# Expert rows by indirect transfers instead of one-hot products, in the first expert stage of a two-block kernel

## The chip, the cores and the metric

The kernel is one program on one core of a Trainium2 chip. The core has a matrix engine (TensorE, PE in the rows; its weight loads are shown as PEld), three elementwise engines (VectorE or DVE, ScalarE or ACT, GpSimd or POOL), a queue engine (SyncE or SP) that issues most transfers, and 16 DMA engines that all queues share. The metric is the device time of one execution in microseconds, as the median of several runs. It is compared with the time of the kernel before the change.

## The reference, cut to what matters

A block of 512 tokens of width 1024 goes through two network blocks one after the other. The first ends with an expert-choice layer: each of 16 experts picks the 64 tokens that its router column rates highest, runs them through a gated network of its own and adds the weighted result back to those tokens.

```
cap = CAP_FACTOR * l // N_EXPERTS                      # 2*512//16 = 64 rows an expert
aff = softmax(h @ w_router)                            # 512 x 16
vals, idx = lax.top_k(swapaxes(aff, 1, 2), cap)        # 16 x 64
xs = h[bidx, idx]
hid = silu(xs @ w_gate) * (xs @ w_up)                  # 64x1024 @ 1024x1024, for each expert
y = (hid @ w_down) * vals[..., None]
x = x + ga2 * zeros_like(h).at[bidx, idx].add(y)
```

Here `h` is the row-normalised `x`, then multiplied by a column scale and shifted (`gs2` and `sh2` in the kernel). The three weight matrices of an expert hold 4 MiB each, so the layer reads 192 MiB. Everything is in float32. The second block, with convolution, attention and another expert layer, follows and isn't touched.

## The kernel before, in words

The program is written as phases. Tiles are drawn from pools with a fixed number of buffers; a planner orders each engine's instructions ahead of time and gives out buffers as they come free in its plan, and each engine and the SP queue then run their lists in order.

`phase_a` computes the first block up to its two branches. `phase_a2` forms the residual `xres` (four tiles of 128 tokens by 1024), its row factors `rs[t]` (L235), the router logits (`logits`, L907 to L941), the 64 best tokens of each expert by eight rounds of max, replace and find index (L990 to L993), and the index and value columns `idxF` and `valF` (L1015, L1016). Keys and values of the second block's cross attention (`mem_k`, `mem_v`, products on L89 to L91) fill TensorE meanwhile. The working tiles of the logits, `xT` and `lgq`, come from a pool tag `ch` with six buffers.

`phase_b` is the first expert stage. Experts go in eight pairs, one in the upper and one in the lower 64 columns of the array, so a tile of rows is 128 rows of a pair. For pair p:

- `gather(p)`: `rows_b` spreads the pair's 128 indices over the partitions by a product (L1038) and compares them with the token numbers (L1041), which gives a one-hot matrix G whose ones carry the row factor `rs4`. A product of `xres` with G (L1079) gives the transposed, normalised rows; `scale_T` (L223) applies column scale and shift.
- `pair_mm` with gate, then up, then down weights (L1068; the last pair's down weights in `last_down`, L1096). Each weight chunk is 256 rows of one expert's matrix, a tile of 128 x 2 x 1024 float32, which is 1 MiB, loaded by L118 on the SP queue. Four steps of two chunks make one `pair_mm`; an expert pair needs 24 chunks and the stage 192.
- `hidden` (L1103 to L1107) multiplies and transposes, `scatter(p)` weights the result (L1122), splits it into a high and a low part (L1124, L1125), brings it back to token order by products with a one-hot matrix P (L96, L97) and adds it (L1130). The sums go into a tile `acc` of their own for pairs 0 to 6, since `gather` still reads `xres`; the last pair adds `acc` and its own rows into `xres`.

The chunks are held in 16 buffers that the loads take in turn: three each of `rawp`, `rawb` and `rawb2`, six of `rawb3`, one of `rawb4`. A load waits until the chunk that was in its buffer has been used. Nine chunks are asked for in `phase_a2` (`preload`), the others as buffers come free. `rawb4` lies on memory that `mem_v` uses until it ends. For the last pair, a tile `gg` for constants of the next phase takes one `rawp` buffer and keeps it.

Of the kernel before, what the change touches and what calls it, by code (L numbers as in the profile page):

```python
# [8 lines left out]
F32 = mybir.dt.float32  # L9
F32R = mybir.dt.float32r  # L10
U32 = mybir.dt.uint32
# [20 lines left out]
NRAW_B3 = 6  # L32
NRAW_B4 = 1
NRAW_D = 4
# [17 lines left out]
def host_constants():  # L52
    c = {}
    c["ident"] = np.eye(128, dtype=np.float32)
    p = np.arange(128)
    c["mask_f"] = np.where(p[:, None] > p[None, :], BIG, 0.0).astype(np.float32)
    c["mask_b"] = np.where(p[:, None] < p[None, :], BIG, 0.0).astype(np.float32)
    s2 = np.zeros((128, 2), np.float32)
    s2[0::32, 0] = 1.0
    s2[1::32, 1] = 1.0  # L60
    c["sel_two"] = s2
    def ang4(r):
        return 2.0 * np.pi * np.outer(p, 4 * p + r) / T
    co, si = (lambda r: np.cos(ang4(r))), (lambda r: np.sin(ang4(r)))
    c["dft_l"] = np.concatenate([co(0), si(0), co(2), si(2), co(1), co(3), si(1), si(3),
                                 -si(1), si(3), co(1), -co(3)], 1).astype(np.float32) * np.float32(T ** -0.5)
    ang = 2.0 * np.pi * np.outer(p, p) / 128
    c["dft_d"] = np.concatenate([np.cos(ang), -np.sin(ang)], 1).astype(np.float32) * np.float32(128 ** -0.5)
    c["mask_n"] = np.where(p[None, :] > p[:, None], -BIG, 0.0).astype(np.float32)
    c["tri"] = np.where(p[:, None] < p[None, :], 1.0, 0.0).astype(np.float32)  # L70
    small = np.zeros((128, 64), np.float32)
    small[:, 8:12] = np.array([4.0, 3.0, 2.0, 1.0])[None, :]
    place = (p[:, None] + 128 * np.arange(4)[None, :])[:, :, None, None] + np.zeros((1, 1, 2, 2))
    place[:, :, 1, 1] += T
    small[:, 16:32] = (place + 1.0).reshape(128, 16)
    c["small"] = small
    c["tokid"] = (p[:, None] + 128 * np.arange(4)[None, :]).astype(np.float32)
    c["iota"] = np.tile(np.arange(T, dtype=np.float32), (128, 1))
    return c


class Builder:
# [156 lines left out]
    def build(self):  # L239
        with ExitStack() as es:  # L240
# [9 lines left out]
            with ExitStack() as right:  # L250
                self.consts()
                with ExitStack() as pb:
                    self.open_b(pb)
                    late = self.phase_a(right)
                    G0 = self.phase_a2(late, pb, right)
                    self.phase_b(pb, right, G0)
                self.raws = [self.rawp] * NRAW
                with ExitStack() as pc:
                    self.phase_c(pc, right)
                with ExitStack() as pd:  # L260
                    self.phase_d(pd)
# [3 lines left out]

    def consts(self):
        nc, I, cst = self.nc, self.I, self.cst
        self.mhalf = cst.tile([128, 1], F32, name="mhalf")
        nc.gpsimd.memset(self.mhalf, -0.5)
        rows1 = cst.tile([128, 128], F32, name="rows1")  # L270
        nc.vector.memset(rows1, 0.0)
# [14 lines left out]

        t = cst.tile([128, 16], F32, name="csil_t")
        nc.scalar.activation(out=t, in_=self.cols1[:, 0:16], func=AF.Tanh, scale=0.5)
        t2 = cst.tile([128, 16], F32, name="csil_t2")
        nc.vector.scalar_tensor_tensor(t2, t, 1.0, self.cols1[:, 0:16], op0=OP.add, op1=OP.mult)  # L290
        self.csil = cst.tile([128, 8, 32], F32, name="csil")
        nc.vector.memset(self.csil, 0.0)
# [45 lines left out]
    def phase_a(self, right):  # L338
        tc, nc, I = self.tc, self.nc, self.I
        cst = self.cst  # L340
        ident = self.ident
        pa, pm, early, late = ExitStack(), ExitStack(), ExitStack(), ExitStack()
        hxp = self.pool(pa, "hxp", 12)
# [503 lines left out]
    def phase_a2(self, late, pb, right):  # L847
# [18 lines left out]
        nc.sync.dma_start(out=wr, in_=I["w_router"][0].rearrange("(k p) c -> p k c", p=128))  # L866
        self.rs4 = cst.tile([128, 4], F32, name="rs4")
        self.tokid = cst.tile([128, 4], F32, name="tokid")
        nc.sync.dma_start(out=self.tokid, in_=I["tokid"])
        affT = self.pa(256, name="affT")  # L870
# [90 lines left out]
        for t in range(4):  # L961
# [4 lines left out]
            ev_x(t, 1, ps)  # L966
            rs[t] = self.row_rstd(sm, sss[t], out=self.rs4[:, t:t + 1])
        logits()
# [41 lines left out]
        V.tensor_tensor(bidx, bidx, two[:, 3, 0:16], op=OP.add)  # L1010
        self.idxF = cst.tile([128, 8], F32, name="idxF")
        self.valF = cst.tile([128, 8], F32, name="valF")
        for par in range(2):
            o = slice(par * 64, par * 64 + 64)
            V.tensor_copy(self.idxF[o, :], bidx.rearrange("c (p two) -> c p two", two=2)[:, :, par])  # L1015
            V.tensor_copy(self.valF[o, :], best.rearrange("c (p two) -> c p two", two=2)[:, :, par])  # L1016
        mem_k()
        G0 = self.rows_b(0)
        mem_v()
        sms.close()  # L1020
        return G0

# [11 lines left out]
    def rows_b(self, p):  # L1034

        V, nc = self.nc.vector, self.nc
        ps = self.pa(128, name="bcI")
        nc.tensor.matmul(ps, self.idxF[:, p:p + 1].to_broadcast([128, 128]), self.ident, start=True, stop=True)  # L1038
        G = self.xsp.tile([128, 4, 128], F32, tag="G", name="G", bufs=1)
        for t in range(4):  # L1040
            V.tensor_scalar(G[:, t, :], ps, self.tokid[:, t:t + 1], self.rs4[:, t:t + 1], op0=OP.is_equal, op1=OP.mult)  # L1041
        return G

    def phase_b(self, pb, right, G0):
        tc, nc, I = self.tc, self.nc, self.I
        ident = self.ident
        V, AC = nc.vector, nc.scalar
        xp = self.pool(pb, "xp", 2)

        acc = xp.tile([128, 4, 1024], F32, name="acc", bufs=1)  # L1050
        if NRAW_B4:
# [18 lines left out]

        def gather(p):
            G = G0 if p == 0 else self.rows_b(p)
            xT = xp.tile([128, 8, 128], F32, tag="xT", name="xT")
            for e in range(2):
                ps = self.pa()
                for q in range(4):
                    k = 4 * e + q
                    for t in range(4):
                        nc.tensor.matmul(ps[:, q * 128:(q + 1) * 128], xres[:, t, k * 128:(k + 1) * 128], G[:, t, :], start=t == 0, stop=t == 3)  # L1079
                self.scale_T(xT[:, 4 * e:4 * e + 4, :].rearrange("p k s -> p (k s)"), ps, self.gs2, self.sh2, 4 * e)  # L1080
            return xT

# [33 lines left out]
        def scatter(p, py):  # L1116
# [3 lines left out]
            for e in range(2):  # L1120
# [5 lines left out]
                for t in range(4):  # L1126
                    ps = self.pa()
                    self.mm2(ps, P[:, t * 128:(t + 1) * 128], (H, L), True, True)
                    c = slice(e * 512, (e + 1) * 512)
                    V.tensor_tensor((acc if p < 7 else xres)[:, t, c], (acc if p else xres)[:, t, c], ps, op=OP.add)  # L1130


        xT = gather(0)
        nc.sync.dma_start(out=self.iota, in_=I["iota"])
# [3 lines left out]
        for p in range(8):  # L1138
            hid = silu(pg)
            nxt = gather(p + 1) if p < 7 else None  # L1140
            hT = hidden(hid, pair_mm(w_u, p, xT))
# [940 lines left out]
```

## Time and profile before

| what | value |
|---|---|
| median of 3 runs | 1710.59 us (1710.18 to 1715.16) |
| the profiled execution | 1714.91 us |
| its span in the profile | 1713.1 us |
| mean granted TensorE clock | 0.969 of full speed |
| busy: PE, DVE, ACT, POOL | 92%, 50%, 36%, 33% of the span |
| read from memory, written | 367.40 MB, 19.93 MB |

The span runs from the first to the last instruction of the profiled execution; 1.8 us of its time lie around it. Times in rows are microseconds from the span's start. The first expert stage runs from about 540 to 1024 us. A busy share of PE is not a share of its peak, because the ends of its pipelined matmuls are modelled. The granted clock is a share of 2.4 GHz, so 0.50 is 1.2 GHz. A float32 matmul of the program is two instructions in the rows.

### The profile page before, as it was taken

The numbers are of one execution on the slowest core, as the hardware profiler recorded it, in microseconds if no ns is written. First come the engines' busy times: TensorE is split into PE (matmuls) and PEld (weight loads), VectorE is DVE, ScalarE is ACT, GpSimd is POOL, SyncE is SP. The second block draws the span as 40 slices with busy tenths as digits, with TensorE's granted clock in tenths as the row PEclk, the third lists the DMA queues.
The fourth block names the chain that finished last, engine by engine and source line by source line (L and its number), as shares of the span: only waits on it lengthen the run. The fifth ranks groups of instructions, "written<-read, shape, count | busy, mean of one in ns | idle before, by whom it ended". The sixth has DMA issues, their size and how long they took to land. (4 is left out here: it accounts for less than half of the span.)

```text
span 1713.1 us, 20867 instructions
## 1 busy us (share of the span) xinstructions
PE 1579.9 (92%) x7702; PEld 1049.7 (61%) x7702; DVE 856.2 (50%) x1595; ACT 613.5 (36%) x1277; POOL 564.9 (33%) x447
## 2 busy tenths in 40 slices
PE   5988999999999999999999978999999989789994
PEld 3766667777776444344344337778666766566663
DVE  4388554423554122022202137997754463667776
ACT  3433354433432000000000034325763354467773
POOL 1213314344513000000000014575443342647765
PEclk9999999999999999999999988999999999889997
DMA  9522412364746999999999983322112328369944
GB/s 302 172 89 91 139 56 93 126 202 148 256 164 245 396 409 409 409 409 409 409 409 409 409 268 124 99 81 91 50 50 85 124 79 327 108 238 346 346 161 165
DMA packets 165548, 381.23 MB, mean 223 GB/s; under 512 B 16302, under 2 KB 74742, under 8 KB 165436
## 3 DMA queue, kind: packets, MB, share of 16 engines
q1 hardware_dynamic: 161116, 371.63, 59.0%
q0 software_dynamic: 4320, 8.16, 1.3%
q8 instruction: 63, 1.03, 0.3%
q14 instruction: 49, 0.40, 0.1%
HBM read 367.40 MB, written 19.93 MB: 226 GB/s over the span
## 5 line engine op out<-in xcount | busy, mean ns | idle before, releaser
L130 POOL TENSOR_TENSOR wL<-raw,wH 128x512 fp32r<-128x512 f32 x220 | 312.0, 1423 | 424.5 <-ACT wH L129 396.1
L129 ACT ACTIVATE wH<-raw 128x512 fp32r<-128x512 f32 x240 | 149.6, 628 | 256.8 <-PE ps L90 149.7
L1068 PE MATMUL ps<-raw,xT 128*64 128x512 f32 x1024 | 240.8, 595 | 0.0
L1068 PEld LDWEIGHTS ps<-raw,xT 128*64 128x64 f32 x1024 | 74.3, 137 | 137.3 <-issue 133.4
L1125 POOL TENSOR_TENSOR yL<-y,yH 128x512 fp32r<-128x512 f32 x14 | 17.9, 1278 | 419.4 <-ACT yH L1124 409.2
L1122 DVE SCALAR_TENSOR_TENSOR y<-ps,valF,ga 128x512 f32<-128x512 f32 x16 | 12.0, 751 | 228.0 <-PE ps L1068 206.8
L91 PE MATMUL ps<-raw,wL 128*128 128x512 f32 (+1 forms) x320 | 120.6, 377 | 2.9 <-POOL wL L130 2.9
L89 PE MATMUL ps<-raw,wH 128*128 128x512 f32 (+1 forms) x320 | 121.3, 379 | 0.7 <-ACT raw L188 0.7
L90 PE MATMUL ps<-raw,wH 128*128 128x512 f32 (+1 forms) x320 | 121.0, 378 | 0.0
L1316 DVE SCALAR_TENSOR_TENSOR cacc<-upad,dwc,cacc 128x512 f32<-128x512 f32 x120 | 118.0, 1036 | 0.9
L1068 PE MATMUL ps<-raw,hidT 128*64 128x512 f32 x448 | 109.3, 594 | 2.8 <-DMA raw<-in_w_down_e 2.8
L89 PE MATMUL ps<-hx,wH 128*128 128x512 f32 x224 | 91.7, 409 | 3.3 <-ACT wH L129 3.3
L91 PE MATMUL ps<-hx,wL 128*128 128x512 f32 x224 | 90.7, 405 | 2.1 <-POOL wL L130 2.1
L1882 DVE TENSOR_TENSOR wL<-raw,wH 128x512 fp32r<-128x512 f32 x96 | 88.4, 976 | 4.6 <-ACT wH L1881 3.3
L1902 POOL TENSOR_TENSOR dL<-raw,dH 128x512 fp32r<-128x512 f32 x64 | 81.6, 1295 | 27.8 <-ACT dH L1901 27.3
L90 PE MATMUL ps<-hx,wH 128*128 128x512 f32 x224 | 90.5, 404 | 0.0
L1124 ACT ACTIVATE yH<-y 128x512 fp32r<-128x512 f32 x16 | 10.0, 626 | 212.7 <-DVE y L1122 212.7
L1107 ACT ACTIVATE hidT<-pa 128x512 f32<-128x512 f32 x16 | 9.6, 597 | 205.0 <-PE pa L1106 205.0
L1068 PEld LDWEIGHTS ps<-raw,hidT 128*64 128x64 f32 x448 | 36.2, 137 | 73.5 <-issue 62.7
L91 PEld LDWEIGHTS ps<-raw,wL 128*128 128x128 f32 x320 | 61.2, 191 | 15.0 <-POOL wL L130 3.4
L89 PEld LDWEIGHTS ps<-raw,wH 128*128 128x128 f32 x320 | 61.4, 192 | 12.2 <-ACT raw L188 1.1
L90 PEld LDWEIGHTS ps<-raw,wH 128*128 128x128 f32 x320 | 61.1, 191 | 11.4 <-issue 0.5
(618 smaller groups left out, 3419.6 us busy)
## 6 DMA issues: line engine op xcount, KB each, us to landing
raw<-in_w_gate_e SPq DMA_DIRECT2D x64, 1024.0 KB
raw<-in_w_up_e SPq DMA_DIRECT2D x64, 1024.0 KB
raw<-in_w_down_e SPq DMA_DIRECT2D x64, 1024.0 KB
raw<-in_w_in SPq DMA_DIRECT2D x34, 1024.0 KB
raw<-in_w_ada SPq DMA_DIRECT2D x24, 1024.0 KB
raw<-in_expert_w_gate SPq DMA_DIRECT2D x32, 512.0 KB
raw<-in_expert_w_up SPq DMA_DIRECT2D x32, 512.0 KB
raw<-in_expert_w_down SPq DMA_DIRECT2D x16, 1024.0 KB
```

Source lines behind the costliest of these rows:

```text
L89: mm(ps, l[0], r[0], start=first, stop=False)
L90: mm(ps, l[0], r[1], start=False, stop=False)
L91: mm(ps, l[1], r[0], start=False, stop=last)
L129: i = self.nc.scalar.activation(out=H, in_=raw_ap, func=AF.Copy)
L130: j = (eng or self.lsub).tensor_tensor(out=L, in0=raw_ap, in1=H, op=OP.subtract)
L1068: nc.tensor.matmul(ps[o, :], act[:, k, o], r[:, q, h * 512:(h + 1) * 512], start=k == 0, stop=k == 7, tile_position=(0, 64 * i))
L1122: V.scalar_tensor_tensor(y, py[e], self.valF[:, p:p + 1], ga2[:, e, :], op0=OP.mult, op1=OP.mult)
L1124: AC.activation(out=H, in_=y, func=AF.Copy)
L1125: (nc.gpsimd if p < 7 else V).tensor_tensor(out=L, in0=y, in1=H, op=OP.subtract)
L1316: V.scalar_tensor_tensor(acc, src, c, acc, op0=OP.mult, op1=OP.add)
L1882: V.tensor_tensor(out=L3, in0=w, in1=H3, op=OP.subtract)
L1902: (nc.gpsimd, V)[DL[i]].tensor_tensor(out=L, in0=src, in1=H, op=OP.subtract)
```

## The change

The rows of an expert pair are no longer formed by products. `phase_a2` multiplies each token tile of `xres` by its row factor on ScalarE and writes the result to a DRAM tensor `xnd` (eight pieces of 128 x 512 from the `ch` buffers, on the SP queue). `rows_b(p)` becomes one indirect transfer that POOL issues: it reads the 128 rows of `xnd` that an integer copy of the indices, `idxU`, names, into a tile `xsb` with one buffer. `gather` transposes that tile by eight products with the identity and then issues the transfer for the next pair. The one-hot matrix G, its comparison and the token numbers go. With `xres` no longer read by `gather`, all pairs add into it and `acc` goes; its 16 KiB per partition become two more buffers for `rawb4` (18 in all). A few start-up constants move to a pool that closes with `phase_a`, and `idxF` and `valF` move to another pool.

```diff
-NRAW_B4 = 1
+NRAW_B4 = 3
...
-            rs[t] = self.row_rstd(sm, sss[t], out=self.rs4[:, t:t + 1])
+            rs[t] = self.row_rstd(sm, sss[t])
+            for e in range(2):
+                c = slice(e * 512, (e + 1) * 512)
+                xn = tc_(name="xn")
+                AC.activation(out=xn, in_=xres[:, t, c], func=AF.Copy, scale=rs[t])
+                nc.sync.dma_start(out=self.xnd[tk, c], in_=xn)
         logits()
...
             V.tensor_copy(self.idxF[o, :], bidx.rearrange("c (p two) -> c p two", two=2)[:, :, par])
+            V.tensor_copy(self.idxU[o, :], self.idxF[o, :])
             V.tensor_copy(self.valF[o, :], best.rearrange("c (p two) -> c p two", two=2)[:, :, par])
+        x0 = self.rows_b(0)
         mem_k()
-        G0 = self.rows_b(0)
         mem_v()
...
     def rows_b(self, p):
 
-        V, nc = self.nc.vector, self.nc
-        ps = self.pa(128, name="bcI")
-        nc.tensor.matmul(ps, self.idxF[:, p:p + 1].to_broadcast([128, 128]), self.ident, start=True, stop=True)
-        G = self.xsp.tile([128, 4, 128], F32, tag="G", name="G", bufs=1)
-        for t in range(4):
-            V.tensor_scalar(G[:, t, :], ps, self.tokid[:, t:t + 1], self.rs4[:, t:t + 1], op0=OP.is_equal, op1=OP.mult)
-        return G
+        x = self.xsp.tile([128, 1024], F32, tag="xsb", name="xsb", bufs=1)
+        self.nc.gpsimd.indirect_dma_start(out=x, out_offset=None, in_=self.xnd[:, :],
+                                          in_offset=bass.IndirectOffsetOnAxis(ap=self.idxU[:, p:p + 1], axis=0),
+                                          bounds_check=511, oob_is_err=False)
+        return x
...
-        acc = xp.tile([128, 4, 1024], F32, name="acc", bufs=1)
...
-        def gather(p):
-            G = G0 if p == 0 else self.rows_b(p)
+        def gather(p, x):
+
             xT = xp.tile([128, 8, 128], F32, tag="xT", name="xT")
             for e in range(2):
                 ps = self.pa()
                 for q in range(4):
-                    k = 4 * e + q
-                    for t in range(4):
-                        nc.tensor.matmul(ps[:, q * 128:(q + 1) * 128], xres[:, t, k * 128:(k + 1) * 128], G[:, t, :], start=t == 0, stop=t == 3)
+                    c = (4 * e + q) * 128
+                    nc.tensor.transpose(ps[:, q * 128:(q + 1) * 128], x[:, c:c + 128], ident)
                 self.scale_T(xT[:, 4 * e:4 * e + 4, :].rearrange("p k s -> p (k s)"), ps, self.gs2, self.sh2, 4 * e)
-            return xT
+            return xT, self.rows_b(p + 1) if p < 7 else None
...
-                    V.tensor_tensor((acc if p < 7 else xres)[:, t, c], (acc if p else xres)[:, t, c], ps, op=OP.add)
+                    V.tensor_tensor(xres[:, t, c], xres[:, t, c], ps, op=OP.add)
```

## Rows read from the trace of the kernel before

**Rows 1.** The page's slices: GB/s that the DMA engines moved, 40 equal slices.

```profile
GB/s 302 172 89 91 139 56 93 126 202 148 256 164 245 396 409 409 409 409 409 409 409 409 409 268 124 99 81 91 50 50 85 124 79 327 108 238 346 346 161 165
```

**Rows 2.** Timeline of PE over one pair: start, duration, engine, line.

```profile
734.82 0.38 PE L1038 MATMUL bcI<-ident,idxF 128*128 128x128 f32 x2
...
737.86 7.41 PE L1079 MATMUL pa<-G,xres 128*128 128x128 f32 x64
...
772.51 13.90 PE L1068 MATMUL ps<-raw,hidT 128*64 128x512 f32 x62
...
793.00 0.38 PE L1038 MATMUL bcI<-ident,idxF 128*128 128x128 f32 x2
```

**Rows 3.** Stretches of 5 us: length, busy by engine, granted clock, DMA share, GB/s.

```profile
530.00:535.00 5.00, 5.00 (x18) 3.85 (x17) 1.93 (x8) 1.62 (x4) 1.79 (x2) 0.69 0.23 89
535.00:540.00 5.00, 5.00 (x29) 4.30 (x28) 0.49 (x1) 1.83 (x3) 2.13 (x2) 1.00 0.01 3
540.00:545.00 5.00, 5.00 (x47) 5.00 (x46) 1.37 (x4) 0.00 (x0) 0.00 (x0) 1.00 0.93 351
545.00:550.00 5.00, 5.00 (x30) 2.44 (x30) 1.37 (x4) 0.00 (x0) 0.00 (x0) 1.00 0.17 68
...
985.00:990.00 5.00, 5.00 (x24) 1.69 (x20) 0.36 (x1) 0.00 (x0) 0.00 (x0) 1.00 1.04 387
...
995.00:1000.00 5.00, 5.00 (x19) 2.92 (x19) 0.00 (x0) 1.19 (x2) 0.00 (x0) 0.50 0.62 230
1000.00:1005.00 5.00, 5.00 (x23) 1.64 (x21) 0.00 (x0) 0.00 (x0) 0.00 (x0) 0.93 0.24 45
...
1015.00:1020.00 5.00, 3.72 (x15) 1.05 (x14) 3.49 (x7) 1.79 (x5) 4.68 (x4) 1.00 1.09 349
```

**Rows 4.** Timeline of the SP queue: issues of weight chunks.

```profile
502.71 3.12 SPq L118 DMA_DIRECT2D raw<-in_w_gate_e  x5
...
539.17 0.39 SPq L118 DMA_DIRECT2D raw<-in_w_up_e  x1
539.65 0.42 SPq L118 DMA_DIRECT2D raw<-in_w_down_e  x1
...
1002.57 0.92 SPq L118 DMA_DIRECT2D raw<-in_w_down_e  x2
```

**Rows 5.** Timeline from the last two pairs to the stage's end; in brackets the wait before.

```profile
966.12 3.65 PE L1068 MATMUL ps<-raw,hidT 128*64 128x512 f32 x12 [0.64 <-DMA raw<-in_w_down_e]
...
997.15 9.68 PE L1096 MATMUL ps<-raw,hidT 128*64 128x512 f32 x34
...
1007.82 3.78 PE L1096 MATMUL ps<-raw,hidT 128*64 128x512 f32 x16 [0.99 <-DMA raw<-in_w_down_e]
...
1013.04 1.19 PE L96 MATMUL pa<-yH,PT 128*128 128x512 f32 x4 [1.44 <-ACT yH L1124]
...
1015.08 3.65 PE L1096 MATMUL ps<-raw,hidT 128*64 128x512 f32 x14
```

**Rows 6.** Groups by line, 540 to 1080 us: busy, mean ns of one, idle before.

```profile
L1106 PE MATMUL pa<-ident,hid 128*128 128x128 f32 x64 | 10.5, 286 | 0.2 <-DVE hid L1103 0.2
...
L1277 ACT ACTIVATE xres<-xg,r 128x512 f32<-128x512 f32 x8 | 5.5, 716 | 0.9 <-POOL r L1265 0.9
```

**Rows 7.** The page's DMA queues: packets, MB, time as share of 16 engines' span.

```profile
q1 hardware_dynamic: 161116, 371.63, 59.0%
q0 software_dynamic: 4320, 8.16, 1.3%
```

**Rows 8.** The tile `xsb` of the second expert stage, gathered indirectly; its transfers' times.

```profile
L1850 POOL DMA_INDIRECT xsb<-hmd,trow x16: 989/1368/1404, 1504.2 to 1632.7; - x16
...
DMA to landing us min/median/max: 4.3/8.0/9.8
```

**Rows 9.** Timeline ahead of the stage: the indices, then the first pair's one-hot products.

```profile
530.30 0.34 DVE L1015 COPY idxF<-bidx 64x8 f32<-64x8 f32 x2
...
538.98 7.31 PE L1079 MATMUL pa<-G,xres 128*128 128x128 f32 x64
```

More of the change, by code (lines that the diff above doesn't have):

```diff
@@ L250, in build @@
             with ExitStack() as right:
-                self.consts()
                 with ExitStack() as pb:
@@ L254, in build @@
                     late = self.phase_a(right)
-                    G0 = self.phase_a2(late, pb, right)
-                    self.phase_b(pb, right, G0)
+                    x0 = self.phase_a2(late, pb, right)
+                    self.phase_b(pb, right, x0)
                 self.raws = [self.rawp] * NRAW
@@ L264, in pool, with consts @@
         return es.enter_context(self.tc.tile_pool(name=name, bufs=bufs, side=side, reuse_waits="tile"))
-    def consts(self):
+    def consts(self, pool):
         nc, I, cst = self.nc, self.I, self.cst
@@ L269, in consts @@
         nc.gpsimd.memset(self.mhalf, -0.5)
-        rows1 = cst.tile([128, 128], F32, name="rows1")
+        rows1 = pool.tile([128, 128], F32, name="rows1")
         nc.vector.memset(rows1, 0.0)
@@ L285, in consts @@
         nc.vector.tensor_copy(self.cols1, ps)
-        t = cst.tile([128, 16], F32, name="csil_t")
+        t = pool.tile([128, 16], F32, name="csil_t")
         nc.scalar.activation(out=t, in_=self.cols1[:, 0:16], func=AF.Tanh, scale=0.5)
-        t2 = cst.tile([128, 16], F32, name="csil_t2")
+        t2 = pool.tile([128, 16], F32, name="csil_t2")
         nc.vector.scalar_tensor_tensor(t2, t, 1.0, self.cols1[:, 0:16], op0=OP.add, op1=OP.mult)
-        self.csil = cst.tile([128, 8, 32], F32, name="csil")
+        self.csil = pool.tile([128, 8, 32], F32, name="csil")
         nc.vector.memset(self.csil, 0.0)
@@ L340, in phase_a @@
         cst = self.cst
+        pa, pm, early, late = ExitStack(), ExitStack(), ExitStack(), ExitStack()
+        self.consts(self.pool(pa, "cs", 1))
         ident = self.ident
-        pa, pm, early, late = ExitStack(), ExitStack(), ExitStack(), ExitStack()
         hxp = self.pool(pa, "hxp", 12)
@@ L866, in phase_a2 @@
         nc.sync.dma_start(out=wr, in_=I["w_router"][0].rearrange("(k p) c -> p k c", p=128))
-        self.rs4 = cst.tile([128, 4], F32, name="rs4")
-        self.tokid = cst.tile([128, 4], F32, name="tokid")
-        nc.sync.dma_start(out=self.tokid, in_=I["tokid"])
+        self.xnd = self.drp.tile([512, 1024], F32, name="xnd")
         affT = self.pa(256, name="affT")
@@ L1010, in phase_a2 @@
         V.tensor_tensor(bidx, bidx, two[:, 3, 0:16], op=OP.add)
-        self.idxF = cst.tile([128, 8], F32, name="idxF")
-        self.valF = cst.tile([128, 8], F32, name="valF")
+        self.idxF = rows.tile([128, 8], F32, name="idxF")
+        self.idxU = rows.tile([128, 8], U32, name="idxU")
+        self.valF = rows.tile([128, 8], F32, name="valF")
         for par in range(2):
@@ L1015, in phase_a2 @@
             V.tensor_copy(self.idxF[o, :], bidx.rearrange("c (p two) -> c p two", two=2)[:, :, par])
+            V.tensor_copy(self.idxU[o, :], self.idxF[o, :])
             V.tensor_copy(self.valF[o, :], best.rearrange("c (p two) -> c p two", two=2)[:, :, par])
+        x0 = self.rows_b(0)
         mem_k()
-        G0 = self.rows_b(0)
         mem_v()
         sms.close()
-        return G0
+        return x0
     def open_b(self, pb):
@@ L1034, in rows_b, with phase_b @@
     def rows_b(self, p):
-        V, nc = self.nc.vector, self.nc
-        ps = self.pa(128, name="bcI")
-        nc.tensor.matmul(ps, self.idxF[:, p:p + 1].to_broadcast([128, 128]), self.ident, start=True, stop=True)
-        G = self.xsp.tile([128, 4, 128], F32, tag="G", name="G", bufs=1)
-        for t in range(4):
-            V.tensor_scalar(G[:, t, :], ps, self.tokid[:, t:t + 1], self.rs4[:, t:t + 1], op0=OP.is_equal, op1=OP.mult)
-        return G
-    def phase_b(self, pb, right, G0):
+        x = self.xsp.tile([128, 1024], F32, tag="xsb", name="xsb", bufs=1)
[3 more added lines that the diff above has]
+        return x
+    def phase_b(self, pb, right, x0):
         tc, nc, I = self.tc, self.nc, self.I
@@ L1129, in scatter @@
                     c = slice(e * 512, (e + 1) * 512)
-                    V.tensor_tensor((acc if p < 7 else xres)[:, t, c], (acc if p else xres)[:, t, c], ps, op=OP.add)
-        xT = gather(0)
+                    V.tensor_tensor(xres[:, t, c], xres[:, t, c], ps, op=OP.add)
+        xT, x = gather(0, x0)
         nc.sync.dma_start(out=self.iota, in_=I["iota"])
@@ L1139, in phase_b @@
             hid = silu(pg)
-            nxt = gather(p + 1) if p < 7 else None
+            if p < 7:
+                nxt, x = gather(p + 1, x)
             hT = hidden(hid, pair_mm(w_u, p, xT))
```

1 line of the change is left out of this document (removed).

## Prediction

> **What bounds the kernel now.** I read the page's slices first, then PE's timeline over one pair, then short stretches at both ends of the expert stage, then the SP queue and the tail. In the slices the reader is to see nine slices in a row at 409 GB/s, from about 600 to 980 us [rows 1]: the DMA engines move weights without a pause. A chunk is 128 x 2 x 1024 x 4 bytes, 1.049 MB, so one takes 2.56 us at that rate, and a pair's 24 chunks take 61.4 us. PE needs less: from one pair's index product to the next is 793.00 - 734.82 = 58.18 us [rows 2]. PE hardly waits all the same, because it starts with 16 loaded buffers and the lead shrinks by only 3.2 us a pair; at 966 us, in the seventh pair's down weights, it is used up and waits for chunks begin (0.64 us) [rows 5]. So the stage is a race that PE and DMA finish nearly together, and a saving on PE is worth only what the DMA engines let through. What counts is when their stream starts, what it carries, and where it has holes.
>
> It has holes at both ends. From 535 to 540 us nothing moves; then two chunks go out at 539.17 and 539.65 [rows 4], 351 GB/s are reached up to 545, and up to 550 it is 68 GB/s, until used buffers come free [rows 3]. At the end, 230 and 45 GB/s stand between 995 and 1005 us [rows 3], since the last two chunks are asked for only at 1002.57 [rows 4]. The ring explains it. Counted through the code, the last eight loads fall on three `rawp` turns, `gg` holds one of the three `rawp` buffers, and so loads wait for a chunk of the same eight. PE waits 0.99 us for them up to 1007.82, multiplies up to 1011.60, waits 1.44 us for the split of the first half and ends its last weight product at 1015.08 + 3.65 = 1018.73 [rows 5].
>
> **The change part by part.** *On PE* a pair loses 7.41 + 0.38 = 7.79 us of index and one-hot products [rows 2] and gains eight transposes. The nearest row, 64 such transposes in 10.5 us [rows 6], gives 0.164 us each, 1.3 us. A pair then needs 58.18 - 7.79 + 1.3 = 51.7 us, 11 us less than the DMA engines. A lead of 18 chunks lasts for 18 / (24/51.7 - 24/62.8) = 220 us, so PE waits for chunks from about 760 us on and the seven savings of 6.5 us, 45 us together, turn into waits. Bounds for what they are worth: nothing, and 45 us. I take nothing but what the stream gives, by the slices at 409.
>
> *DVE* loses four comparisons a pair, hidden under PE before and after. The sums in place cost what the sums into `acc` cost: as many instructions of the same shape.
>
> *On the DMA engines* seven row transfers of 128 x 4 KiB, 0.524 MB, fall into the stream (the first is over before it). At 409 GB/s one costs 1.28 us. The software queue took 1.3% of 1713.1 us for 8.16 MB [rows 7], 2.73 us a MB, so 1.43 us by that row. I take 1.4, seven make 9.8 us; the bounds are 0, if they slip in for nothing, and 10.0. I stay at the top, since nothing in nine full slices is spare. Their latency is hidden: in the second expert stage such a transfer lands 4.3 to 9.8 us after its issue and costs POOL 1.4 us [rows 8], and each is issued about a pair, 50 us, ahead.
>
> *The two buffers.* All three of `rawb4` lie on memory that `mem_v` holds to its end, as the one before did, so they can be asked for at 539 us and not earlier. At that time four chunks go out in place of two: 14 chunks are loaded, 178 are left, and the stream runs without the hole up to 550. PE's first product starts some 5 us earlier than at 546 (7.31 us of one-hot products [rows 9] against 1.3 of transposes and a wait for their scaling), and frees buffers from about 545, ahead of the fourth chunk's end at 551. At the end, the ring of 18 puts only one `rawp` turn among the last eight loads, with two `rawp` buffers free of `gg`: the hole between 995 and 1005 goes.
>
> *The stream's end.* It starts at 540.7 (351 of 409 GB/s fill 4.3 us of the 5 up to 545 [rows 3]). 178 x 2.56 = 455.7 us of chunks, 9.8 of rows, and 8 x 0.15 = 1.2 us because the last pair's down chunks of 2 KiB pieces go at 387 GB/s [rows 3]: the last chunk lands at 1007.4. Before, 176 chunks from 550 took 450.6 us, plus 6.6 us lost in the hole (5 x (1 - 230/409) + 5 x (1 - 45/409)) plus 1.2: 1008.4, against a wait for them that ended at 1007.82 [rows 5]. So the working holds for before within 1 us, and the gain of both holes is nearly eaten by the rows.
>
> *The tail.* What sets the end is the last chunk of the seventh pair's down weights: behind it PE has a long run of its own. It lands eight chunks of 2.71 and eight of 2.56 us before the last, at 1007.4 - 42.2 = 965.2; its step of 16 instructions, at 13.90 / 62 = 0.224 us [rows 2], ends at 968.8. Before, that step ended at 966.12 + 3.65 = 969.77, and from there to 1018.73 it took 48.96 us, 2.43 of them the two waits (0.99 and 1.44) that came from late chunks in the wrong order [rows 5]. Without them 46.5 us remain, and the stage ends at 1015.3, 3.4 us earlier. The landing itself would allow 1007.4 + 3.6 = 1011.0, so PE's own run decides.
>
> *Ahead of the stage* ScalarE does eight more scalings of 0.72 us [rows 6]. Six lie in idle time; the last two, of the fourth token tile, stand before the router logits and can hold them by up to 1.4 us. `idxU` adds two DVE copies behind 530.64 (two like them took 0.34 us [rows 9]), and the first transfer, from about 531.3, lands by 536 to 541; PE is busy with `mem_v` to 538.98 [rows 9], and 2 us later would still cost the stream nothing, since four chunks keep it busy to 551. The 2.1 MB written to `xnd` go mostly into stretches where little moves. Between 0 and 1.4 us, I take 0.5, as the logits wait mostly for PE.
>
> Sum: 3.4 - 0.5 = 2.9 us. The profiled execution (1714.91, of which 1713.1 is span) would go to 1712.0; its median stands 4.3 us lower, so the forecast is 1710.6 - 2.9 = **1707.7 us**. A change under 0.3%, 5.1 us, can't be told from none here.
>
> **The rivals.** *Slower: the logits wait for the rows' writes.* The writes of the fourth tile are issued at about 508 us on the SP queue, behind the preloaded chunks that it sends out from 502.71 [rows 4]. Six chunks at 2.56 us occupy the engines to about 520, so these two `ch` buffers come free at 521, not 510. If the planner gives one of them to a tile of the logits, the logits end 12 us later; `mem_v` behind them on PE ends later too, and with it the start of the stream: 12 - 3 = 9 us slower, 1719.6. It decides if a tile that is wanted before 521 draws such a buffer; four others are free, which speaks against it. The Trainium skill (DMA: Bandwidth & Descriptors, "Queues, rings and completion order") says that a queue's descriptors are consumed in ring order on each DMA engine, which is what this rival needs; no row here shows a small write behind chunks.
>
> *The clock falls.* A starved PE works 3.6 us of each 5.1 in its weight steps. The granted clock was 0.69 and 0.50 (1.2 GHz) in two stretches [rows 3], and around the second the 34 instructions of the last pair took 0.285 us each in place of 0.224 [rows 5]. Against it: from 1015 to 1020, at 3.72 of 5 us busy, it stayed 1.00 [rows 3]. During the starved pairs a slow spell is hidden by 11 us of wait; in the tail one of 10 us costs 5: 1712.7, two 1717. The Trainium skill (TensorE: Matmul & The Clock Gate, "HAM oscillation") warns of just this, a loop whose wait for each weight slice exceeds its products; here the wait, 1.5 us, is shorter than the products, so by that rule it stays a lesser case.
>
> *Faster: the rows cost the stream nothing.* Then it ends 9.8 us earlier, and all behind it: 1697.9. Nine slices at the same 409 speak against it. *Faster: no slow spell in the tail.* The 34 instructions at 0.224 us save 2.1 us more, and an earlier first half hides its scatter: 1704 to 1705. *Faster: PE sets the pace after all* and its 45 us come through: about 1660; only if 409 GB/s is no limit.
>
> **How the numbers follow.** Forecast, a gain of 1 to 5 us, 0.53. Rows for nothing, or in part, 0.09; no slow spell in the tail 0.17; PE's pace 0.02. Clock 0.09 (two thirds of it within 0.3%). Logits 0.10. Faster by over 0.3%: 0.09 + 0.02 + 0.17 = 0.28. Slower: 0.10 + 0.03 = 0.13. The rest, 0.59, is within. The range reaches into the free rows and into the slower cases: 1700 to 1716, and leaves out about 0.08 below and 0.10 above. The forecast's own range is 1705.5 to 1709.6.
>
> **What would show it.** Right: 409 GB/s from 541 without a break to about 1005; no loads asked for after 990 but those of the next phase; PE's waits for chunks beginning near 760 and totalling some 40 us; the last weight product ending near 1015. Wrong: a stream that ends before 1000 or runs above 409; PE waiting for `xsb`; logits after 515 us; a granted clock of 0.50 between 700 and 1000.

## The result, and the profile after

The changed kernel is slower: 1721.24 us (median of 8 runs, 1717.19 to 1723.71) against 1713.19 us for the kernel before in the same comparison, ratio 1.0051 with a 95% interval of 1.0038 to 1.0064. One of the eight executions of the kernel before took 3977.87 us and is left out of the ratio; the median of the other seven is 1712.24 us. A second comparison gave 1.0053 (1.0035 to 1.0072). The forecast was 1707.7 us, a ratio of about 0.998, with a range up to 1716. So the change costs some 8.7 us (0.0051 of the time) where 2.9 were to be gained: 11.6 us to explain.

The profiled execution of the changed kernel took 1717.19 us, the shortest of its eight. Much of what looks good in it is chance: soon after 220 us, long ahead of the expert stage, it was already 3.9 us ahead of the profile of before, and a second profile of the same code was 1.0 us behind there. So I compare stretches, and not ends: the same instructions of ScalarE and VectorE are matched in two traces, and I look where the distance between their start times grows.

The expert stage first. Stretches of the changed kernel, with the columns of [rows 3]:

```profile
535.00:540.00 5.00, 4.91 (x27) 3.87 (x26) 0.88 (x3) 1.74 (x4) 1.28 (x1) 0.98 0.47 114
540.00:545.00 5.00, 5.00 (x24) 1.76 (x26) 2.16 (x7) 0.96 (x1) 1.02 (x1) 1.00 0.94 360
545.00:550.00 5.00, 5.00 (x26) 1.67 (x24) 0.00 (x0) 0.00 (x0) 0.00 (x0) 1.00 1.02 412
...
995.00:1000.00 5.00, 4.80 (x40) 4.26 (x40) 0.29 (x1) 3.00 (x6) 0.00 (x0) 0.94 1.05 385
1000.00:1005.00 5.00, 5.00 (x18) 1.58 (x20) 0.00 (x0) 0.58 (x1) 0.00 (x0) 0.71 1.04 387
```

Both holes of [rows 3] are closed: 412 GB/s in place of 68 from 545 to 550, and 385 and 387 in place of 230 and 45 from 995 to 1005. Between them the stream runs at 409 without a break, as in [rows 1]. TensorE has the time that was forecast to turn into waits. Its timeline over one pair, as in [rows 2]:

```profile
729.54 0.60 PE L1078 MATMUL pa<-ident,xsb 128*128 128x128 f32 x4
...
766.67 4.50 PE L1068 MATMUL ps<-raw,hidT 128*64 128x512 f32 x16 [0.57 <-DMA raw<-in_w_down_e]
771.79 4.55 PE L1068 MATMUL ps<-raw,hidT 128*64 128x512 f32 x16 [0.62 <-DMA raw<-in_w_down_e]
776.90 4.49 PE L1068 MATMUL ps<-raw,hidT 128*64 128x512 f32 x16 [0.57 <-DMA raw<-in_w_down_e]
782.03 3.65 PE L1068 MATMUL ps<-raw,hidT 128*64 128x512 f32 x12 [0.63 <-DMA raw<-in_w_down_e]
...
792.26 0.60 PE L1078 MATMUL pa<-ident,xsb 128*128 128x128 f32 x4
```

From one pair's transposes to the next are 62.72 us, where it was 58.18 [rows 2]: TensorE does 6.5 us less work (by the forecast's sum) and takes 4.5 us longer, at the pace of the stream. How long it waits is not one number. The waits from 480 to 1030 us (us in total, times, longest), in the rows of the products and in those of their weight loads:

```profile
PE ps L1068 <- DMA raw<-in_w_down_e: 14.3, 24, 0.6
PE ps L1068 <- DMA raw<-in_w_gate_e: 6.5, 11, 0.7
PEld ps L1068 <- DMA raw<-in_w_down_e: 38.7, 36, 1.5
PEld ps L1068 <- DMA raw<-in_w_gate_e: 22.3, 27, 1.5
```

They add up to 20.8 us by the products, whose ends are modelled and reach into a wait, and to 61.0 by the weight loads; the forecast had some 40. The row transfers are never waited for by TensorE. Their tile, with the times of its transfers (in [rows 8] they are 4.3, 8.0 and 9.8 us):

```profile
L1041 POOL DMA_INDIRECT xsb<-xnd,idxU x8: 990/1003/1228, 533.5 to 858.8; - x8
...
DMA to landing us min/median/max: 4.9/7.5/9.2
```

The tail, beside [rows 5]:

```profile
970.20 3.65 PE L1068 MATMUL ps<-raw,hidT 128*64 128x512 f32 x12 [0.63 <-DMA raw<-in_w_down_e]
...
999.88 9.40 PE L1095 MATMUL ps<-raw,hidT 128*64 128x512 f32 x34
...
1012.05 7.08 PE L1095 MATMUL ps<-raw,hidT 128*64 128x512 f32 x30
```

The stage's last weight product ends at 1019.13, against 1018.73 before [rows 5] and a forecast of 1015.3. The run behind the seventh pair's down weights is 1.2 us shorter than forecast (45.3 us from 973.85, forecast 46.5); it starts late, at 973.85 in place of 968.8.

The other loss lies where I had not looked, 85 us ahead of the stage. The tile of the router's weights in the changed kernel (who issued what, and who waited), and TensorE's timeline there:

```profile
L859 DVE MEMSET wr<- x1: 272/272/272, 444.9 to 444.9; 128x256 f32 x1
L865 SPq DMA_DIRECT2D wr<-in_w_router x1: 458/458/458, 446.5 to 446.5; - x1
...
who waited for it (us, times):
  PE cw L885: 1.9, 1
```

```profile
451.64 0.40 PE L88 MATMUL ps<-wH,mH 128*128 128x512 f32 x1
453.92 1.93 PE L885 MATMUL cw<-wr,sh 128*128 128x16 f32 x16 [1.88 <-DMA wr<-in_w_router]
```

The same tile in the kernel before:

```profile
L860 DVE MEMSET wr<- x1: 272/272/272, 380.5 to 380.5; 128x256 f32 x1
L866 SPq DMA_DIRECT2D wr<-in_w_router x1: 373/373/373, 380.8 to 380.8; - x1
...
who waited for it (us, times):
  DVE cw L889: 0.9, 1
```

Before, these weights were loaded 70 us ahead of their use. Now the memset that opens the tile comes at 444.9, the load goes out at 446.5 and TensorE stands still for it; behind the pause its granted clock is 0.67 from 455 to 460. These stretches, and then the second of them in the kernel before, where it was 1.00:

```profile
450.00:455.00 5.00, 3.12 (x19) 2.43 (x17) 4.33 (x7) 1.71 (x4) 1.90 (x2) 1.00 1.05 369
455.00:460.00 5.00, 5.00 (x20) 4.15 (x20) 3.67 (x7) 2.71 (x5) 2.33 (x2) 0.67 1.03 381
```

```profile
455.00:460.00 5.00, 5.00 (x24) 4.10 (x24) 3.63 (x6) 3.44 (x7) 1.82 (x2) 1.00 1.04 381
```

No line that computes anything was edited there. The new pool for the start-up constants is opened first in `phase_a`, so all tiles of that phase move up by some 1.6 KiB per partition (the sizes of the tiles that moved). The reading that the runs below test: `wr`, which comes behind them in the same memory, now lies on a buffer that `phase_a` uses almost to its end. The trace shows no addresses, so which buffer that is stays an inference.

### The profile page after: what moved, and what is told of

Its sections match the earlier page's. It is cut to its first block, busy times and chain, and to the rows that moved or that the text cites. A ratio compares the mean times of both kernels' runs of the same rounds, so it can differ in the third digit from the quotient of the medians.

```text
span 1715.4 us, 19996 instructions
## 1 busy us (share of the span) xinstructions
PE 1560.4 (91%) x7238; PEld 1004.1 (59%) x7238; DVE 844.6 (49%) x1565; ACT 619.1 (36%) x1285; POOL 572.7 (33%) x455
## 5 line engine op out<-in xcount | busy, mean ns | idle before, releaser
L1068 PE MATMUL ps<-raw,xT 128*64 128x512 f32 x1024 | 254.5, 597 | 6.7 <-DMA raw<-in_w_gate_e 6.5
L1068 PEld LDWEIGHTS ps<-raw,xT 128*64 128x64 f32 x1024 | 80.6, 136 | 159.1 <-issue 135.2
L1068 PE MATMUL ps<-raw,hidT 128*64 128x512 f32 x448 | 130.2, 602 | 14.3 <-DMA raw<-in_w_down_e 14.3
L1068 PEld LDWEIGHTS ps<-raw,hidT 128*64 128x64 f32 x448 | 39.9, 136 | 99.7 <-issue 59.5
```

Of the source, the lines that this page charges most:

```text
L1068: nc.tensor.matmul(ps[o, :], act[:, k, o], r[:, q, h * 512:(h + 1) * 512], start=k == 0, stop=k == 7, tile_position=(0, 64 * i))
```

## The experiments

All ratios are against the kernel before, run beside each kernel on the same chip. There are four sets, each on a chip of its own: a0, x1, x2, x3; b1, y1, g1, h1; z0, b2, k1, y2; x4, k2. Differences between ratios are firmest within a set. "Drift" is the growth of the distance between the matched instructions of the profile and that of before: from 400 to 480 us (the router's weights) and from 520 to 1040 us (the expert stage). The second column depends by up to 0.6 us on which instructions near its two ends are taken.

| kernel | ratio (95%) | drift 400 to 480 | drift 520 to 1040 |
|---|---|---|---|
| z0_before_again | one run | 0.6 | -2.4 |
| the changed kernel, first profile | 1.0051 (1.0038 to 1.0064) | 3.4 | 0.8 |
| a0_after_again | 1.0053 (1.0035 to 1.0072) | 3.9 | 1.3 |
| x1_consts_above | 1.0024 (1.0014 to 1.0034) | -0.4 | 1.2 |
| x2_rows_once | 1.0009 (0.9996 to 1.0021) | 3.7 | -6.5 |
| x3_pe_back | 1.0048 (1.0033 to 1.0064) | 5.3 | 3.7 |
| b1_consts_moved | 0.9989 (0.9975 to 1.0004) | 3.9 | -1.7 |
| y1_one_buffer | 1.0032 (1.0020 to 1.0044) | 0.4 | 2.6 |
| g1_skip_turn | 0.9979 (0.9968 to 0.9990) | 0.0 | -2.5 |
| h1_first_pair | 0.9985 (0.9972 to 0.9998) | 0.6 | -5.0 |
| b2_consts_above | 0.9968 (0.9955 to 0.9980) | -0.4 | -0.8 |
| k1_both_edits | 0.9956 (0.9942 to 0.9970) | -0.4 | -3.3 |
| y2_rows_once_above | 0.9979 (0.9970 to 0.9988) | 0.3 | -7.9 |
| x4_pad_96 | 1.0045 (1.0032 to 1.0058) | 0.8 | 2.8 |
| k2_first_pair | 0.9990 (0.9981 to 0.9999) | 0.3 | -5.1 |

Four kernels have the stage of before (the first profile, 0 by definition, z0, b1 and b2); their mean is -1.2. So the profile on which the forecast rests had a stage about 1.2 us longer than that mean, within a spread of 2.4 us among the four.

**The changed kernel again**, unchanged, for the scatter.

> The changed kernel once more, beside the others of this set. Two theories of its 0.5%. Late router weights plus stream: in phase_a2 the load of the router weights is issued near 446 us instead of 381, TensorE waits 1.9 us for it and then runs at a low clock (3.3 us in all), and the expert stage ends no earlier than before because the DMA stream carries seven row transfers more. Then this profile shows the same: the wait for the router weights near 453, and a stage that ends 0 to 2 us later than before, counted from the point 480 us. Rival, a chance of layout in the start-up: the profile of the changed kernel shows the first phase 3.9 us shorter than before, and the time would scatter by as much from run to run; then the median lies anywhere between 1717 and 1724.

1722.5 us against 1711.68, ratio 1.0053: the loss is no chance.

**The layout.** The pool of constants is opened behind the phase's other pools, so that nothing moves up:

```diff
-        self.consts(self.pool(pa, "cs", 1))
-        ident = self.ident
         hxp = self.pool(pa, "hxp", 12)
...
         sm = self.pool(pa, "sm", 2)
+        self.consts(self.pool(pa, "cs", 1))
+        ident = self.ident
```

> The changed kernel with the start-up constants' pool opened after the other pools of phase_a instead of ahead of them, so that the tiles of phase_a lie where they lay before. Theory: the router weights' tile overlays memory that phase_a uses to its end only because that pool shifted everything; then its load is issued near 380 again, the wait of 1.9 us and the low clock behind it go, and the time falls by 3 to 3.5 us against the changed kernel. Rival: the planner put the load late for another reason, such as the new writes in the SP queue; then the load stays near 446 and nothing changes.

1.0024: 0.29% less than a0 in the same comparison, 5.0 us. The load of the router's weights is back at its place in the SP queue:

```profile
381.74 0.37 SPq L865 DMA_DIRECT2D wr<-in_w_router  x1
```

**The same move alone, on the kernel before.**

```diff
-                self.consts()
...
         pa, pm, early, late = ExitStack(), ExitStack(), ExitStack(), ExitStack()
+        self.consts(self.pool(pa, "cs", 1))
+        ident = self.ident
```

> The kernel before with one edit of the change alone: the start-up constants go into a pool that is opened first in the first phase and closes with it, nothing else. Theory (layout): every tile of that phase moves up, the router's weight tile comes to lie on a tile that is in use until about 445 us, its load is issued at about 446 in place of 381 and TensorE waits some 1.9 us for it near 454, with a dip of the granted clock behind: 3 to 5 us slower, ratio 1.0018 to 1.003. Rival (the delay came from the eight new pieces of rows in the same pool, not from the layout): ratio 1.000 within 0.001 and the load is issued at 381.

The mechanism came as expected; the total did not (1.0018 to 1.003 were expected). The late load and the wait are there:

```profile
455.33 2.58 PE L888 MATMUL cw<-wr,sh 128*128 128x16 f32 x16 [1.65 <-DMA wr<-in_w_router]
457.74 0.77 PE L90 MATMUL ps<-wL,mH 128*128 128x512 f32 x1
458.32 0.63 PE L91 MATMUL ps<-wH,mL 128*128 128x512 f32 x1
```

The products behind the wait take 0.63 us in place of 0.39, and the drift is 3.9 us. But the ratio is 0.9989: between 1040 and 1320 us this kernel wins 4.7 us back, in a phase that no edit touches. There most of its products of 128x512 take 389 to 394 ns, nearly all without a wait, in place of 394 to 400. One group from 1060 to 1200 us, first of the kernel before, then of this one:

```profile
L89 PE MATMUL ps<-wH,raw 128*128 128x512 f32 x32 | 12.6, 395 | 0.0
```

```profile
L89 PE MATMUL ps<-wH,raw 128*128 128x512 f32 x32 | 12.4, 389 | 0.0
```

**Both sides of the layout apart.** On the kernel before, the pool behind the others, as in x1:

> The kernel before with the constants' pool opened after the phase's other pools: the constants leave the top of the memory as in b1_consts_moved (0.9989), but no tile of the first phase moves. b1's profile lost 3.9 us between 440 and 480 and ran its products in the third phase at 389 to 394 ns in place of 395 to 400, some 3 us less in all. Theory (two effects of the layout that cancel there): here only the gain is left, ratio 0.9955 to 0.997, products of the third phase at 389 to 394 ns. Rival (those 389 ns were a matter of that run, and the 3.9 us come back somewhere): ratio 0.9985 to 1.0005, products at 395 or more.

0.9968, with no drift at 480 and the faster products (389 to 391 ns). So b1 held two effects of opposite sign, and b2 against b1 (0.0021, 3.6 us) prices the router's weights a second time, though across two sets. Over the fifteen profiles the split is clean: 3.4 to 5.3 us in the five with the pool opened first, -0.4 to 0.8 in the ten others.

**The row transfers.** Only the first pair's rows are fetched; every pair multiplies these, so the output is not the layer's:

```diff
-            return xT, self.rows_b(p + 1) if p < 7 else None
+            return xT, x
```

> The changed kernel without the row transfers of pairs 1 to 7: all pairs use the rows of the first, so the output is not that of the layer. Stream theory: the seven transfers' 3.67 MB are all that falls away, 9.2 us of the DMA engines, TensorE was waiting for chunks anyway, and the stage ends 8 to 10 us earlier, 1711 to 1713 in all. Rival, transfers hidden: no change, about 1721. Rival, TensorE's own run at the end decides: 3 us at most.

1.0009, 0.44% or 7.5 us below a0; in the stage 7.3 us below the changed kernel's first profile and 7.8 below a0's. The stage's pace shows the same: from the last down product of the third pair to that of the fourth are 62.7 us in the changed kernel and 61.4 to 61.5 without the rows, here and in y2 below. So a pair's rows cost 1.2 to 1.3 us of the stream, where 1.4 were forecast.

**Both repaired.** The same edit on x1; again the output is not the layer's:

> The changed kernel with both of its costs taken out: constants' pool opened after the others (1.0024 alone), and one row transfer in place of eight (1.0009 alone; all pairs multiply the rows of the first, so the output is not the layer's). If the layout's cost and the rows' cost add, the ratio is 1.0009 - 0.0029 = 0.998 (0.997 to 0.999): then the rest of the change is worth 3.4 us, about what was forecast for the whole. Rival (one hides the other): 1.001, as x2_rows_once.

0.9979, where adding the two gave 0.998. The two costs add, as far as these ratios tell: 0.0030 for the layout (y2 against x2) and 0.0045, 7.7 us, for the rows (y2 against x1), 9.1 us by the stage's drift. (In the profiles of x2 and y2 some 6 us are lost again behind 1320 us, where the second block works on other values; their ratios may understate the rows' price.) What remains, the shorter work on TensorE, the earlier start and the two buffers, is worth 3.6 us by y2's ratio and 6.7 by its stage (-7.9 against the mean of -1.2).

**TensorE's saving.** The products that the change removed are put back as 64 dummy instructions a pair (four products of 128x128 for each transpose, overwritten by it):

```diff
                     c = (4 * e + q) * 128
+                    for t in range(4):
+                        nc.tensor.matmul(ps[:, q * 128:(q + 1) * 128], x[:, c:c + 128], x[:, c:c + 128], start=t == 0, stop=t == 3)
                     nc.tensor.transpose(ps[:, q * 128:(q + 1) * 128], x[:, c:c + 128], ident)
```

> The changed kernel with 64 matmul instructions a pair put back on TensorE, as many and as large as the one-hot products that were removed (their result is overwritten). Stream theory: the waits for chunks absorb 11 us a pair, so seven times 7.4 us vanish in them and the time stays within 2 us of the changed kernel; only the first pair's 7.4 us come at a place without waits, and four queued chunks cover them. Rival, TensorE sets the pace: 50 to 59 us slower, above 1770.

1.0048, against 1.0053 without them. The groups of TensorE from 540 to 1000 us, first of the changed kernel, then of this one (busy, mean ns of one, and the idle time before them):

```profile
L1068 PE MATMUL ps<-raw,hidT 128*64 128x512 f32 x448 | 130.2, 602 | 14.3 <-DMA raw<-in_w_down_e 14.3
```

```profile
L1068 PE MATMUL ps<-raw,hidT 128*64 128x512 f32 x448 | 111.9, 596 | 3.4 <-DMA raw<-in_w_down_e 3.2
L1079 PE MATMUL pa<-xsb 128*128 128x128 f32 x512 | 64.7, 275 | 0.0
```

The 64.7 us of added work cost nothing by the ratio: they fill the waits. (The waits in these rows shrink by less than that, since the modelled ends of the products shrink too: 130.2 to 111.9 us here, and 254.5 to 239.2 for the gate and up weights.) By its one profile the stage is 2.4 to 2.9 us longer than in the two of the changed kernel, little more than two profiles of one code can differ.

**The two buffers.** x1 with one buffer in `rawb4` (`NRAW_B4 = 1`):

> The changed kernel with the constants' pool opened after the others (as in the run above at 1.0024) and with one buffer in rawb4 in place of three, so 16 in all. Theory (stream): two chunks in place of four can go out at 539, and the last eight loads fall on three rawp turns again, so the hole near 1000 comes back: 3 to 7 us slower than with three, ratio 1.004 to 1.0065. Rival (the two buffers are worth nothing, since TensorE now starts and frees buffers 5 us earlier, and a stream that is starved by nobody has no use for more lead): ratio 1.002 to 1.003.

1.0032, 1.4 us over x1, and 1.4 us in the stage's drift. That is between theory and rival, and the intervals of the two kernels overlap, so it isn't clear of nothing; the 3 to 7 us of the theory didn't come. The mechanism did: 225 and 173 GB/s from 1000 to 1010 us, and the wait in the last pair is back.

```profile
1000.00:1005.00 5.00, 5.00 (x21) 1.87 (x21) 0.00 (x0) 1.04 (x2) 0.00 (x0) 0.66 0.61 225
1005.00:1010.00 5.00, 5.00 (x24) 1.70 (x20) 0.00 (x0) 0.00 (x0) 0.00 (x0) 1.00 0.51 173
```

```profile
1011.14 3.78 PE L1095 MATMUL ps<-raw,hidT 128*64 128x512 f32 x16 [0.88 <-DMA raw<-in_w_down_e]
```

**The hole closed without the change.** The kernel before, with a ring that leaves out one `rawp` turn behind `gg`:

```diff
                 gg = self.gg = self.rawp.tile([128, 2, 1024], F32, tag="raw", name="raw")
+                i = self.nraw % len(self.raws)
+                self.raws, self.nraw = self.raws[i:] + self.raws[:i], 0
+                self.raws.remove(self.rawp)
```

> The kernel before, with one edit of three lines: behind the tile gg the ring leaves out one rawp turn, so that none of the last eight loads waits for a chunk of the same eight. All row work as before. Theory (stream): the hole from 995 to 1005 goes, and the two waits of 0.99 and 1.44 us in the tail with it: 2 to 3.5 us faster, ratio 0.998 to 0.9988. Rival (the tail is set by TensorE's own run and the clock there, the waits only move): ratio 1.000 within 0.001.

0.9979, 3.6 us faster, though only 1.3 us of it by the drift of the stage against the mean of the four above. The hole is gone in its stretches:

```profile
995.00:1000.00 5.00, 5.00 (x17) 1.57 (x18) 0.00 (x0) 0.60 (x1) 0.00 (x0) 0.65 1.05 388
1000.00:1005.00 5.00, 4.70 (x20) 1.26 (x16) 0.75 (x1) 0.23 (x1) 0.00 (x0) 1.00 1.04 378
```

**The first pair's rows alone.** g1 with an indirect transfer for pair 0, into the tile that later holds `ga2`; pairs 1 to 7 keep their one-hot products:

> The kernel before with the ring edit of g1_skip_turn, and with the indirect transfer for the first pair's rows alone (into the tile that later holds the scale ga2); pairs 1 to 7 keep their one-hot products, acc, the constants and the one buffer of rawb4 stay. So the expert stage starts as early as in the changed kernel, and no row transfer falls into the stream. Theory (stream): first gate product near 540.5 in place of 546.2, the stream from 541 to about 1000, the stage's end 5 to 7 us earlier than before: ratio 0.996 to 0.9975. Rival (the eight scalings and writes ahead of the logits, 2 us, and one preloaded chunk fewer, 2.6 us, take most of that back): ratio 0.998 to 0.9995.

The stage is 2.5 us shorter than in g1, but the medians don't show it: 0.9985 against 0.9979, intervals that overlap. That is the rival's range and not the theory's, but against g1 it stays unclear.

**Before again**, for a second profile:

> The kernel before, unchanged, for a second profile of it: how far two profiles of the same code differ. From the other runs: the stretch up to 220 us, where the granted clock rises, differs by up to 4 us between runs; from 220 to 1000 us two profiles of the same code should keep their distance within 0.5 us; the rest of the stage and the phase behind it within 2. If the stretch from 440 to 520 differs by more than 1 us, the 3.9 us read there from single profiles of other kernels mean nothing.

0.6 us from 400 to 480 us, just over the 0.5 expected, and far from the 3.4 of the router's weights. The stage, at -2.4, spreads a little more than the 2 expected.

**Candidates.** b2 with the ring edit of g1:

> b2_consts_above with the ring edit of g1_skip_turn (0.9979), a candidate that beats both kernels. If the two add: 0.9979 plus whatever b2_consts_above gives, so 0.994 to 0.995 by its theory and 0.997 to 0.9985 by its rival. Nothing of the row work is changed.

0.9956 (0.9942 to 0.9970), 1703.71 us: the lowest ratio here, clearly below the kernel before and the changed one (its interval overlaps b2's), and its rows are formed as before. The two edits added would give 0.9947, within its interval. With the first pair's rows by transfer on top:

> k1_both_edits (0.9956) with the first pair's rows by indirect transfer, as in h1_first_pair: a second candidate. Theory (stream): the expert stage starts 5 us earlier and carries no rows, 2 to 4 us faster than k1, ratio 0.993 to 0.9945. Rival (as h1 against g1: one preloaded chunk fewer takes it back): 0.995 to 0.9965.

0.9990: expected gain missed. The stage is 1.8 us shorter than in k1, but the products behind it take 395 ns again, and from 1040 to 1320 us it wins 1.2 us where k1 wins 4.7.

**The fast products.** x1 with 96 bytes more in the permanent pool:

```diff
+        nc.vector.memset(cst.tile([128, 24], F32, name="pad"), 0.0)
```

> x1_consts_above (the changed kernel, constants' pool opened after the others, 1.0024) with a dummy tile of 96 bytes per partition in the permanent pool, where idxF, valF, rs4 and tokid stood before, so that all later pools start where they start in b2_consts_above (0.9968). Theory (the duration of the third phase's products hangs on where its tiles start): the products of 1060 to 1200 us take 389 to 394 ns in place of 395 to 396, and the ratio falls by some 0.0020 to 0.0030, to 0.9994 to 1.0005. Rival (what b1, b2 and k1 have and the changed kernel lacks is something else): 395 to 396 ns and 1.0015 to 1.003.

1.0045, products mostly at 395 to 396 ns (three small groups at 388 to 394). My theory falls: the start of the pools alone doesn't decide. It is also a warning: x4 and x1 differ by 0.2% though their profiles agree within 1.6 us in the stage, so differences of that size between separate comparisons are not to be leaned on.

## Why the prediction was wrong, step by step

**What I left out: where tiles lie.** The prediction weighed each edit by its instructions. The move of the constants has none, and so it got no step, not even at nothing. It cost 3.4 to 5.3 us by the drift, 3.6 to 5.1 by three pairs of ratios (a0 and x1, b1 and b2, x2 and y2); x4, which has the same repair, came out only 0.08% below a0, so the size is known to a few us, the mechanism by its rows. This is the first failed step. Its mechanism was shown from both sides: undone in the changed kernel, and made alone in the one before (by the rows and the drift; in b1's total the faster products hide it).

**"14 chunks are loaded, 178 are left": the stream was undersized.** This is the second failed step. From 538 us to the end of the last pair's up weights, at 990.2, the packets in the trace add up to 183.9 MB; at 409 GB/s that is 449.6 us, a start at 540.6, as forecast (540.7). The prediction's working puts 181.9 MB there: 170 chunks of 1.049 MB and 3.67 MB of rows. The 2.0 MB too many take 4.9 us. The step on the seventh pair's down weights ends 5.05 us late, and the last chunk's pieces land at 1011.9 us in place of 1007.4. 1.05 MB are one chunk: 13 were loaded by 538 us, not 14. The SP queue:

```profile
511.87 0.87 SPq L117 DMA_DIRECT2D raw<-in_w_gate_e  x1
520.66 0.37 SPq L117 DMA_DIRECT2D raw<-in_w_down_e  x1
...
538.86 5.68 SPq L117 DMA_DIRECT2D raw<-in_w_up_e  x5
```

Of the three loads into buffers that come free between 511 and 530 us, which before go out in a row, only two come ahead of the loads that wait for `mem_v`; the third goes out at 538.9 or later. I read this as the third standing in the queue behind those: I counted "what is loaded" by buffers and forgot that the queue runs in order. Of the five in the last row, three go out by 540 us and two only at 543.7, behind the stage's first products; four at 539 were forecast. The other 0.9 MB are 0.26 MB of instruction loads and 2-KiB pieces of the last chunks that overtake. That the extra chunk alone is worth 2.6 us was not tried by itself.

**The rows in the stream: right.** Forecast 9.8 us (1.4 each); measured 7.3 to 9.1 in the stage, 7.5 to 7.7 by ratios. The rival "rows cost nothing" falls. But its time, 1697.9, was off as well: without the rows, and with the layout mended, y2 takes 1709.27, in which the stream's surplus, the profile's long stage and the 6 us lost behind 1320 us stay.

**TensorE's 45 us are worth nothing: right** within what the ratio can show, by x3. **The two buffers: right in kind, small in size.** They close the hole at 1000 us. That is worth some 1.4 us if anything (y1), though the two slow stretches lost the stream 6.6 us by the forecast's working.

**The sum against one profile.** The stage of that profile was 1.2 us longer than the mean of four. I took the whole gain from a median that stood 4.3 us below that profile; 1.2 us of it the usual execution may not have to give. Added up: the forecast was 2.9 us faster. The layout takes 3.4 to 5.3. The stage came out 0.8 to 1.3 longer where 3.4 shorter was forecast, so it takes 4.2 to 4.7: the stream's 4.9, less some of the 1.2 that the shorter run at the end gave back. With 1.2 for the profile that makes 5.9 to 8.3 us slower, where 8.7 were measured. The rest is not explained.

**The rivals.** "Logits wait for the writes" came in small and cost nothing that shows. One tile waited 0.9 us for a write of `xnd`. Counted from the router's product, the last logits product starts 57.7 us later in the changed kernel and 55.5 in the one before: 2.2 us, where up to 1.4 were forecast. But the last products of `mem_v` are no later, and the stage's first weight product comes at 539.99 in place of 546.21. "The clock falls" didn't come: between 600 and 980 us the granted clock is 1.00 in every stretch, though from 756 us on TensorE waits in every 5.1 us, 0.6 us by the rows of the products and up to 1.5 by those of the weight loads, against 3.6 us of products (16 at 0.224). The Trainium skill (TensorE: Matmul & The Clock Gate, "HAM oscillation") describes a loop that falls to the lower clock at each weight slice because its wait is longer than its products; the wait here was the shorter, and the trace agrees that such waits left the clock alone. The chance of 0.13 for slower lay on these two; both mechanisms that decided were missing from the list.

## What to carry to other kernels

A new pool, or one opened earlier, moves every tile behind it: before and after such an edit, compare for each tile when its first write and its load are issued, since a load that was 70 us early can become the one that the matrix engine waits for. Where a stage is bound by its transfers, count the bytes that it still has to move when it starts, in the order of the queue and not by free buffers; work taken off TensorE was worth nothing here (x3), and rows fetched again through the same DMA engines were paid nearly in full (7.3 to 9.1 us, where their bytes at 409 GB/s take 9.0). Take the sum against more than one profile of the kernel before, since stages of the same code differed by up to 2.4 us here.

## What the runs showed of the hardware that was not expected

One wait of 1.58 to 1.88 us on TensorE in full work, followed by 16 narrow products (128x16) of 1.9 to 2.6 us, cost 3.4 to 5.3 us in five profiles, since the products behind them ran at 0.63 us (1.2 GHz) in place of 0.39 (2.4 GHz) for some microseconds. In b1 the granted clock was 0.64 from 455 to 460 and 0.68 to 465; in the kernel before, with the same narrow products and no such wait, it was 1.00. Waits of 0.6 us in the products' rows, up to 1.5 in the weight loads', in every 5.1 us over 200 us, left the granted clock at 1.00.

Long rows of products of 128x512 that wait for nothing ran in one of two ways in the third phase (1060 to 1200 us): 0.226 us from one start to the next in b1, b2 and k1, and 0.231 to 0.234 us in the kernel before and the others. It followed the kernel and not the chip, and was worth some 3 to 5 us. Padding by 96 bytes didn't bring it about, so its cause stays open.
